# Row sums of the attention weights from a column of ones, the maximum negated where it is formed, and one cast on ScalarE

## The chip, the cores and the metric

The kernel runs on one core of one Trainium2 chip. A core has TensorE (PE; PEld is its weight load), VectorE (DVE), ScalarE (ACT), GpSimd (POOL) and SyncE (SP), which run side by side and wait for each other by semaphores. The metric is the device time of one execution in microseconds. All times below come from three timed runs of the kernel before and from one profiled execution of it.

## The reference

Two layers over 1024 latent tokens and 256 context tokens of width 1024. The first layer mixes tokens by Fourier transforms and long convolutions, the second by attention, and each ends with a gated feed-forward block. The change lies in the attention of the second layer alone: 16 heads of width 64; a query sees the keys in a window of its 16 x 64 grid, with a position bias, and all context keys, under one softmax.

```python
s_loc = einsum(q_r, k_b) * scale + bias          # masked outside the window
s_ctx = einsum(q_r, kc) * scale
s = concatenate([s_loc, s_ctx], axis=-1)
p = softmax(s, axis=-1)
o = einsum(p_loc, v_b) + einsum(p_ctx, vc)
```

## The kernel before

The program is written as Python generators, and a scheduler puts the instructions of each engine in an order by times that it works out itself; so the order on an engine is not the order of the source, and a small edit can move many instructions. Each engine then runs its own list from front to back.

**Precision.** Operands are kept as a high and a low part, and a product is three matmuls: high x high, high x low, low x high. Keys and queries are fp32r (an fp32 word rounded for TensorE), weights of the softmax and values fp16.

**Preparation.** `attn_prep(pr, u)` makes what a pair of heads `pr` (of 8) needs: keys `kk`, `kc` and queries `qs` by the linear products in `lin` (24 matmuls of 512 columns each, into PSUM tiles named `pq`), split in the lines L1989, L1990, L2002 and L2003; and values. `value(c)` loads a 128-row chunk of values (c = 0 to 3 for the four column windows of the grid, 512 columns; c = 4 for the context, 256 columns), scales it by `self.vs` into the fp16 high part on ScalarE (L1970) and takes the low part on VectorE (L1971). Both parts lie in one tile of 1024 fp16 columns. `weights` loads a weight block and splits it (L326 on ScalarE, L328 on VectorE).

**Items.** `attn_item` handles one head, half of the rows and two of the four column windows: 64 items in all (4 for each head: `hf` 0 and 1, `c0` 0 and 2). Its three stages are:

1. Scores: matmuls against 256 context keys into `pctx`, and against 384 window keys into two more PSUM tiles (`ps`). The bias tiles `g` (128 x 384) are loaded from `in_bias` by the SP queue; their pool has 4 buffers.
2. Softmax: L2072 takes the maximum of the context scores, L2075 adds the bias and takes the maximum over both (one custom instruction and a read of its accumulator), L2077 negates it, L2078 and L2080 take the exponential on ScalarE and also sum each row (each with a read of ScalarE's accumulator), L2081 adds the two sums and L2082 takes the reciprocal. Then the weights are transposed: the local ones by TensorE (L2095), split by L2098 (ScalarE, high part) and L2099 (VectorE, low part). The context's weights go another way in the first 48 items (`cross`): L2089 casts them to fp16 on VectorE, L2090 takes the low part on GpSimd, L2091 transposes both with a DMA of the SP queue. In the last 16 items they are transposed by TensorE like the others.
3. Values: 30 matmuls of 64 columns (15 for each of two windows) into one PSUM tile `o`; L2125 scales the result by the reciprocal on ScalarE. After every four items `attn_out` transposes (L2135), splits (L2137, L2138) and stores it.

`attention` walks over the items so that stage 1 of an item, stage 2 of the one before and stage 3 of the one before that stand together, and puts pieces of the next pair's preparation between them ("fill"); during the last pairs the fill is the first part of the output projection (L2390). PSUM tiles `ps` rotate over 6 banks here.

Of the kernel before, what the change touches and what calls it, by code (L numbers as in the profile page):

```python
# [12 lines left out]
F16 = mybir.dt.float16  # L13
# [5 lines left out]
P = 128  # L19
# [217 lines left out]
class Builder:  # L237
# [1664 lines left out]
    def values(self, u):  # L1902
# [31 lines left out]
        nc.vector.tensor_scalar(self.vs, m1, 8192.0, None, op0=MUL)  # L1934
        nc.vector.tensor_scalar(self.vsi, m2, 1.0 / 8192.0, None, op0=MUL)

    def attn_prep(self, pr, u):

        nc, a = self.nc, self.a
        kk = [self.S4(F32R), self.S4(F32R)]
        kc = self.S2(F32R)
        qs, vt = {}, []

        def lin(wh, wl, pc, acc, view=lambda x: x):
            acc[pc] = self.PQ()
            for kb in range(KB):
                for w, part in ((wh, 0), (wh, 1), (wl, 0)):  # L1950
                    self.mm(acc[pc][:, :WID[pc]], w[:, kb * P:(kb + 1) * P], view(u.ap(part, kb, pc)),
                            kb == 0 and w is wh and part == 0, kb == KB - 1 and w is wl)
                yield WID[pc] / 1024

        def by_chunk(x):
            return x.rearrange("p (r h c) -> p h r c", r=8, h=4)

        def value(c):
            st = self.T()
            w = 512 if c < 4 else 256  # L1960
            if c < 4:
                src = self.vd[0:LAT].rearrange("(g r w) c -> r w g c", g=4, r=4)
                for r in range(4):
                    self.ld(st[r * 32:r * 32 + 32].rearrange("p (g c) -> p g c", g=4),
                            src[r, KSTART[c]:KSTART[c] + 32, :, pr * P:(pr + 1) * P])
            else:
                self.ld(st[:, :w].rearrange("p (j c) -> p j c", j=2),
                        self.vd[LAT:LAT + CTX, pr * P:(pr + 1) * P].rearrange("(j p) c -> p j c", j=2))
            t = self.S2(F16, 1024)
            nc.scalar.activation(t[:, :w], st[:, :w], AF.Copy, scale=self.vs)  # L1970
            nc.vector.scalar_tensor_tensor(t[:, w:2 * w], st[:, :w], self.vs, t[:, :w], op0=MUL, op1=SUB)  # L1971
            vt.append(t)

        if pr == 0:
            self.aw = self.weights(a["wk"][0])
        acc = {}
        wk = self.aw
        for pc in (0, 1, 2):
            for i, s in enumerate(lin(*wk, pc, acc)):
                if i == 3:  # L1980
                    value(len(vt))
                if pc == 1 and i == 6:
                    wq = self.weights(a["wq"][pr])
                yield s
            w = WID[pc]
            for hd in (0, 1):
                own, other = slice(hd * 64, hd * 64 + 64), slice(64 - hd * 64, 128 - hd * 64)
                dst = kk[hd][:, pc * 512:pc * 512 + w] if pc < 2 else kc[:, hd * 256:hd * 256 + 256]
                nc.scalar.copy(dst[own], acc[pc][own, :w])  # L1989
                nc.vector.tensor_tensor(dst[other], acc[pc][own, :w], dst[own].bitcast(F32), SUB)  # L1990
        nxt = None
        for pc in (0, 1):
            for i, s in enumerate(lin(*wq, pc, acc, by_chunk)):
                if i == 3:
                    value(len(vt))
                if pc == 1 and i == 3 and pr < 7:
                    nxt = self.weights(a["wk"][pr + 1])
                yield s
            for hd in (0, 1):
                own, other = slice(hd * 64, hd * 64 + 64), slice(64 - hd * 64, 128 - hd * 64)  # L2000
                qh, ql = self.S2(F32R), self.S2(F32R)
                nc.scalar.mul(qh[own], acc[pc][own], 0.125)  # L2002
                nc.vector.scalar_tensor_tensor(ql[own], acc[pc][own], 0.125, qh[own].bitcast(F32), op0=MUL, op1=SUB)  # L2003
                for t in (qh, ql):
                    self.ldr(t[other].bitcast(F32), t[own].bitcast(F32))
                qs[(hd, pc)] = (qh, ql)
        self.aw = nxt
        self.prep[pr] = (qs, kk, kc, vt)
        yield 0.1
# [37 lines left out]
    def attn_item(self, head, hd, hf, c0, qs, kk, kc, vt, osb, out, cross):  # L2047
# [20 lines left out]
            loc.append(ps)  # L2068
        yield
        st = self.pt.tile([P, 16], F32, tag="st", name=self.nm("st"))  # L2070
        cm, mx, nm, s1, s2, rv = (st[:, 2 * i:2 * i + 2] for i in range(6))
        nc.vector.tensor_reduce(cm, pctx.rearrange("p (i k) -> p i k", i=2), axis=AX, op=MAX)  # L2072
        pc = self.T()
        for i in (0, 1):
            nc.vector.tensor_tensor_reduce(bias[i], loc[i][:, :384], bias[i], 1.0, cm[:, i:i + 1], ADD, MAX,  # L2075
                                           mx[:, i:i + 1])
            nc.vector.tensor_scalar(nm[:, i:i + 1], mx[:, i:i + 1], -1.0, None, op0=MUL)  # L2077
            nc.scalar.activation(pc[:, i * 256:i * 256 + 256], pctx[:, i * 256:i * 256 + 256], AF.Exp,  # L2078
                                 bias=nm[:, i:i + 1], accum_out=s2[:, i:i + 1])
            nc.scalar.activation(bias[i], bias[i], AF.Exp, bias=nm[:, i:i + 1], accum_out=s1[:, i:i + 1])  # L2080
        nc.vector.tensor_tensor(s1, s1, s2, ADD)  # L2081
        nc.vector.reciprocal(rv, s1)  # L2082
        pts = [None] * 3
        turns = [(1, bias[0], 3), (0, pc, 4), (2, bias[1], 3)]
        if cross:

            turns.pop(1)
            x, pts[0] = self.TK(F16, 1024), self.S2(F16, 1024)
            nc.vector.tensor_copy(x[:, :512], pc)  # L2089
            nc.gpsimd.tensor_tensor(x[:, 512:], pc, x[:, :512], SUB)  # L2090
            nc.sync.dma_start_transpose(pts[0].rearrange("p (n c) -> p n c", c=P), x)  # L2091
        for k, src, n in turns:
# [12 lines left out]
        for i in (0, 1):  # L2105
            c = c0 + i
            ops = []
            for g in range(3):
                gg = hf + g
                v = vt[c][:, gg * P + hd * 64:gg * P + hd * 64 + 64]  # L2110
                vl = vt[c][:, 512 + gg * P + hd * 64:512 + gg * P + hd * 64 + 64]
                ops.append((pts[1 + i], g, v, vl))
            for j in range(2):
                v = vt[4][:, j * P + hd * 64:j * P + hd * 64 + 64]
                vl = vt[4][:, 256 + j * P + hd * 64:256 + j * P + hd * 64 + 64]
                ops.append((pts[0], 2 * i + j, v, vl))
            oo = o[:, i * 64:(i + 1) * 64]
            for n, (t, j, v, vl) in enumerate(ops):
                ph, pl = t[:, j * P:(j + 1) * P], t[:, 512 + j * P:512 + (j + 1) * P]
                self.mm(oo, ph, v, n == 0, False)  # L2120
                self.mm(oo, ph, vl, False, False)
                self.mm(oo, pl, v, False, n == 4)
        for i in (0, 1):
            c = c0 + i
            nc.scalar.activation(osb[hf][:, c * P + hd * 64:c * P + hd * 64 + 64], o[:, i * 64:(i + 1) * 64],  # L2125
                                 AF.Copy, scale=rv[:, i:i + 1])
        if out is not None:
            self.attn_out(out, hf, osb[hf])
# [434 lines left out]
```

## Time and profile before

| | |
|---|---|
| median of 3 runs | 2956.7 us (2954.18 to 2958.66) |
| profiled execution | 2957.89 us, of which 2956.0 us are its span |
| granted TensorE clock, mean | 0.984 |
| busy in the span | PE 2832.5 us, DVE 2092.7, ACT 1330.1, POOL 529.2 |
| attention, 1774 to 2240 us of the span | 466 us for 64 items |
| busy in it | PE 430.09 us, DVE 359.52, ACT 315.69, POOL 118.02 |

The span is the time from the first to the last instruction; the 1.89 us between it and the time lie around it. A row of a group gives busy time, the mean of one instruction in ns, and after a second bar the idle time of the engine just before such instructions, with what ended it. A PE row shows a matmul from its issue to its modelled end, so rows overlap and a row's mean is longer than the pace at which matmuls follow each other. DVE and ACT rows overlap a little too. A row of `DVE_READ_ACCUMULATOR2_ANT` or `ACTIVATION_READ_ACCUMULATOR` is the second half of an instruction that also sums or compares along the row.

### The profile page before, as it was taken

The page shows a single profiled execution, that of the slowest core. Times are in us where ns is not written, and L with a number is a line of the kernel's source. Part 1 is how long each engine was busy: PE and PEld are TensorE (multiplying, and loading weights), DVE is VectorE, ACT ScalarE, POOL GpSimd, SP SyncE. Part 2 cuts the span into 40 slices and gives each one's busy share as a digit, 9 for nine tenths or more (in the row PEclk, how much of TensorE's full clock was granted, in tenths as well). Part 3 has the DMA queues.
Part 4 walks back from the last instruction along what each step waited for, and adds up shares of the span by engine and source line. Part 5 has one row for each costly group of instructions (what it writes and reads, how often), then busy time and mean ns, then how long its engine had stood idle before and what let it go on. Part 6 is the DMA issues. An engine that isn't in the chain of part 4 may idle for free. (4 is left out here: it accounts for less than half of the span.)

```text
span 2956.0 us, 44485 instructions
## 1 busy us (share of the span) xinstructions
PE 2832.5 (96%) x15704; PEld 2363.7 (80%) x15704; DVE 2092.7 (71%) x3950; ACT 1330.1 (45%) x2490; POOL 529.2 (18%) x820
## 2 busy tenths in 40 slices
PE   8899898899999999999999999999999999999998
PEld 3678787788799888888888888788877688888886
DVE  6765666858777888966777437888777877764555
ACT  4543323543454333333455336677665533333433
POOL 2112012351100221222120002232212022111000
PEclk9999999999999999999999999999999999999999
DMA  9664433566556555659984345676756266434653
GB/s 336 219 210 161 144 102 127 185 222 225 199 176 199 193 202 202 219 189 323 309 305 153 129 130 154 174 183 168 221 169 226 75 240 227 168 111 167 227 194 128
DMA packets 303917, 568.41 MB, mean 192 GB/s; under 512 B 83144, under 2 KB 129930, under 8 KB 303694
## 3 DMA queue, kind: packets, MB, share of 16 engines
q1 hardware_dynamic: 242750, 373.11, 39.7%
q0 software_dynamic: 58640, 188.26, 17.8%
q10 hardware_dynamic: 2304, 4.20, 0.4%
q8 instruction: 124, 2.03, 0.3%
q14 instruction: 99, 0.81, 0.1%
HBM read 415.49 MB, written 119.80 MB: 181 GB/s over the span
## 5 line engine op out<-in xcount | busy, mean ns | idle before, releaser
L1605 PE MATMUL ps<-s,s 128*128 128x512 f32 x2008 | 498.3, 391 | 6.4 <-DVE s L1496 4.7
L1605 PEld LDWEIGHTS ps<-s,s 128*128 128x128 f32 x2008 | 377.6, 188 | 88.3 <-DVE s L1496 6.3
L322 PE MATMUL ps<-s,wh 128*128 128x256 f32 (+1 forms) x1584 | 358.7, 329 | 3.5 <-ACT wh L326 3.4
L322 PE MATMUL pq<-s,wh 128*128 128x512 f32 (+1 forms) x1040 | 316.2, 381 | 9.8 <-DVE s L1990 4.7
L322 PEld LDWEIGHTS ps<-s,wh 128*128 128x128 f32 x1584 | 265.8, 192 | 29.6 <-ACT wh L326 4.7
L322 PE MATMUL ps<-s,s 128*128 128x64 f16 (+3 forms) x2780 | 243.8, 241 | 31.1 <-DVE s L2099 8.8
L1777 PE MATMUL ps<-s,s 128*128 128x512 f32 (+1 forms) x1000 | 259.6, 383 | 3.1 <-DVE s L328 3.0
L328 DVE TENSOR_TENSOR wl<-ws,wh 128x1024 fp32r<-128x1024 f32 (+1 forms) x142 | 170.0, 1198 | 127.5 <-ACT wh L326 123.0
L326 ACT CAST wh<-ws 128x1024 fp32r<-128x1024 f32 (+1 forms) x142 | 145.8, 1027 | 241.2 <-PE ps L322 91.8
L326 ACT CAST s<-s 128x1024 fp32r<-128x1024 f32 (+2 forms) x184 | 168.1, 940 | 191.3 <-DMA s<-d 162.6
L322 PE MATMUL ps<-s,wl 128*128 128x256 f32 (+1 forms) x792 | 238.4, 327 | 2.7 <-DVE wl L328 2.7
L322 PEld LDWEIGHTS pq<-s,wh 128*128 128x128 f32 x1040 | 190.8, 191 | 47.5 <-DVE s L1990 5.9
L326 ACT CAST s<-t 128x512 fp32r<-128x512 f32 (+1 forms) x213 | 121.9, 587 | 220.9 <-PE ps L1605 81.2
L328 DVE TENSOR_TENSOR s<-s,s 128x1024 fp32r<-128x1024 f32 (+2 forms) x162 | 185.5, 1177 | 49.4 <-ACT s L326 46.9
L1777 PEld LDWEIGHTS ps<-s,s 128*128 128x128 f32 x1000 | 184.5, 188 | 41.2 <-DVE s L328 4.6
L322 PE MATMUL ps<-s,mat 128*128 128x512 f32 x714 | 180.3, 402 | 18.1 <-ACT s L326 10.9
L322 PE MATMUL pq<-s,wl 128*128 128x512 f32 (+1 forms) x520 | 196.3, 379 | 1.3 <-DVE wl L328 1.3
L328 DVE TENSOR_TENSOR s<-t,s 128x512 fp32r<-128x512 f32 (+1 forms) x213 | 136.9, 653 | 78.9 <-ACT s L326 51.0
L1605 PE MATMUL ps<-s,wh 128*128 128x512 f32 x608 | 189.1, 390 | 0.0
L322 PEld LDWEIGHTS ps<-s,mat 128*128 128x128 f32 x714 | 135.6, 193 | 54.9 <-ACT s L326 13.5
L322 PEld LDWEIGHTS ps<-s,s 128*128 128x128 f32 (+1 forms) x860 | 133.9, 196 | 45.3 <-ACT s L326 10.9
L322 PEld LDWEIGHTS ps<-s,wl 128*128 128x128 f32 x792 | 148.8, 191 | 16.4 <-DVE wl L328 3.6
(439 smaller groups left out, 5614.9 us busy)
## 6 DMA issues: line engine op xcount, KB each, us to landing
s<-d SPq DMA_DIRECT2D x283, 256.0 KB, 3.8
s<-in_down SPq DMA_DIRECT2D x150, 256.0 KB, 4.1
d<-s POOLq DMA_DIRECT2D x137, 256.0 KB, 3.3
s<-in_ada_w POOLq DMA_DIRECT2D x64, 512.0 KB, 5.2
d<-tk POOLq DMA_DIRECT2D x98, 256.0 KB, 3.6
g<-in_bias SPq DMA_DIRECT2D x128, 192.0 KB, 3.1
ws<-in_up SPq DMA_DIRECT2D x44, 512.0 KB, 3.9
d<-g POOLq DMA_DIRECT2D x87, 256.0 KB, 3.1
```

What stands on the lines that cost most here:

```text
L322: self.nc.tensor.matmul(o, l, r, start=st, stop=sp)
L326: self.last_hi = nc.scalar.copy(hi, src).ins
L328: self.last_lo = eng.tensor_tensor(lo, src, hi.bitcast(F32), SUB).ins
L1605: nc.tensor.matmul(ps, x[:, sl], y, start=first and j == 0 and x is wh and y is xh, stop=j == 3 and x is wl, skip_group_check=True)
L1777: m = nc.tensor.matmul(acc[j][:, c0:c1], x[:, sl], y[:, xs], start=first and k == 0, stop=last and k == 2, skip_group_check=True)
```

## The change

Four things are done, all in the attention.

- The high part of the values gets a column of ones behind every 64 columns: `blocks(t, 65, ...)` is a view of blocks of 65, L1984 of the new file sets the ones on GpSimd, and the matmuls with the high part (two of three) have 65 columns. Column 64 of `o` is then the row's sum of weights. ScalarE no longer sums the rows, the addition L2081 is gone, and the reciprocal (now L2133) reads the sums out of PSUM after the value matmuls.
- Four blocks of 65 more columns don't fit, so `low_parts` says where the low part of a chunk lies: for c < 4 mostly in its own tile, with the last one or two blocks in the tile of the context's values. The low part of such a chunk is taken by two instructions (L1987) where it was one. The five tiles are allocated together at the start of `attn_prep`.
- The maximum is negated where it is formed: the reduction gives the negative (L2088), the custom instruction multiplies the sum by -1 and takes the minimum (L2091), the exponential of the local weights gets a scale of -1. L2077 is gone.
- The cast of the context's weights for the DMA transpose moves from VectorE (L2089) to ScalarE (L2102).

```diff
--- before.py
+++ after.py
@@ -1934,6 +1934,14 @@
         nc.vector.tensor_scalar(self.vs, m1, 8192.0, None, op0=MUL)
         nc.vector.tensor_scalar(self.vsi, m2, 1.0 / 8192.0, None, op0=MUL)
 
+    def low_parts(self, vt, c):
+
+        if c == 4:
+            return [(0, 4, vt[4][:, 260:516])]
+        if c < 3:
+            return [(0, 6, vt[c][:, 520:904]), (6, 2, vt[4][:, 516 + c * P:516 + c * P + P])]
+        return [(0, 7, vt[3][:, 520:968]), (7, 1, vt[4][:, 900:964])]
+
     def attn_prep(self, pr, u):
 
 
@@ -1955,21 +1963,29 @@
         def by_chunk(x):
             return x.rearrange("p (r h c) -> p h r c", r=8, h=4)
 
-        def value(c):
+        vt[:] = [self.S2(F16, 1024) for _ in range(5)]
+        filled = []
+
+        def value():
+            c = len(filled)
+            filled.append(c)
             st = self.T()
-            w = 512 if c < 4 else 256
+            n = 8 if c < 4 else 4
             if c < 4:
                 src = self.vd[0:LAT].rearrange("(g r w) c -> r w g c", g=4, r=4)
                 for r in range(4):
                     self.ld(st[r * 32:r * 32 + 32].rearrange("p (g c) -> p g c", g=4),
                             src[r, KSTART[c]:KSTART[c] + 32, :, pr * P:(pr + 1) * P])
             else:
-                self.ld(st[:, :w].rearrange("p (j c) -> p j c", j=2),
+                self.ld(st[:, :256].rearrange("p (j c) -> p j c", j=2),
                         self.vd[LAT:LAT + CTX, pr * P:(pr + 1) * P].rearrange("(j p) c -> p j c", j=2))
-            t = self.S2(F16, 1024)
-            nc.scalar.activation(t[:, :w], st[:, :w], AF.Copy, scale=self.vs)
-            nc.vector.scalar_tensor_tensor(t[:, w:2 * w], st[:, :w], self.vs, t[:, :w], op0=MUL, op1=SUB)
-            vt.append(t)
+            blocks = lambda x, w, b0, k: x[:, b0 * w:(b0 + k) * w].rearrange("p (b c) -> p b c", c=w)
+            t = vt[c]
+            nc.gpsimd.memset(blocks(t, 65, 0, n)[:, :, 64:65], 1.0)
+            nc.scalar.activation(blocks(t, 65, 0, n)[:, :, :64], blocks(st, 64, 0, n), AF.Copy, scale=self.vs)
+            for b0, k, lo in self.low_parts(vt, c):
+                nc.vector.scalar_tensor_tensor(blocks(lo, 64, 0, k), blocks(st, 64, b0, k), self.vs,
+                                               blocks(t, 65, b0, k)[:, :, :64], op0=MUL, op1=SUB)
 
         if pr == 0:
             self.aw = self.weights(a["wk"][0])
@@ -1978,7 +1994,7 @@
         for pc in (0, 1, 2):
             for i, s in enumerate(lin(*wk, pc, acc)):
                 if i == 3:
-                    value(len(vt))
+                    value()
                 if pc == 1 and i == 6:
                     wq = self.weights(a["wq"][pr])
                 yield s
@@ -1992,7 +2008,7 @@
         for pc in (0, 1):
             for i, s in enumerate(lin(*wq, pc, acc, by_chunk)):
                 if i == 3:
-                    value(len(vt))
+                    value()
                 if pc == 1 and i == 3 and pr < 7:
                     nxt = self.weights(a["wk"][pr + 1])
                 yield s
@@ -2068,25 +2084,22 @@
             loc.append(ps)
         yield
         st = self.pt.tile([P, 16], F32, tag="st", name=self.nm("st"))
-        cm, mx, nm, s1, s2, rv = (st[:, 2 * i:2 * i + 2] for i in range(6))
-        nc.vector.tensor_reduce(cm, pctx.rearrange("p (i k) -> p i k", i=2), axis=AX, op=MAX)
+        cm, mn, rv = (st[:, 2 * i:2 * i + 2] for i in range(3))
+        nc.vector.tensor_reduce(cm, pctx.rearrange("p (i k) -> p i k", i=2), axis=AX, op=MAX, negate=True)
         pc = self.T()
         for i in (0, 1):
-            nc.vector.tensor_tensor_reduce(bias[i], loc[i][:, :384], bias[i], 1.0, cm[:, i:i + 1], ADD, MAX,
-                                           mx[:, i:i + 1])
-            nc.vector.tensor_scalar(nm[:, i:i + 1], mx[:, i:i + 1], -1.0, None, op0=MUL)
+            nc.vector.tensor_tensor_reduce(bias[i], loc[i][:, :384], bias[i], -1.0, cm[:, i:i + 1], ADD, MIN,
+                                           mn[:, i:i + 1])
             nc.scalar.activation(pc[:, i * 256:i * 256 + 256], pctx[:, i * 256:i * 256 + 256], AF.Exp,
-                                 bias=nm[:, i:i + 1], accum_out=s2[:, i:i + 1])
-            nc.scalar.activation(bias[i], bias[i], AF.Exp, bias=nm[:, i:i + 1], accum_out=s1[:, i:i + 1])
-        nc.vector.tensor_tensor(s1, s1, s2, ADD)
-        nc.vector.reciprocal(rv, s1)
+                                 bias=mn[:, i:i + 1])
+            nc.scalar.activation(bias[i], bias[i], AF.Exp, bias=mn[:, i:i + 1], scale=-1.0)
         pts = [None] * 3
         turns = [(1, bias[0], 3), (0, pc, 4), (2, bias[1], 3)]
         if cross:
 
             turns.pop(1)
             x, pts[0] = self.TK(F16, 1024), self.S2(F16, 1024)
-            nc.vector.tensor_copy(x[:, :512], pc)
+            nc.scalar.copy(x[:, :512], pc)
             nc.gpsimd.tensor_tensor(x[:, 512:], pc, x[:, :512], SUB)
             nc.sync.dma_start_transpose(pts[0].rearrange("p (n c) -> p n c", c=P), x)
         for k, src, n in turns:
@@ -2106,23 +2119,21 @@
             c = c0 + i
             ops = []
             for g in range(3):
-                gg = hf + g
-                v = vt[c][:, gg * P + hd * 64:gg * P + hd * 64 + 64]
-                vl = vt[c][:, 512 + gg * P + hd * 64:512 + gg * P + hd * 64 + 64]
-                ops.append((pts[1 + i], g, v, vl))
+                ops.append((pts[1 + i], g, c, 2 * (hf + g) + hd))
             for j in range(2):
-                v = vt[4][:, j * P + hd * 64:j * P + hd * 64 + 64]
-                vl = vt[4][:, 256 + j * P + hd * 64:256 + j * P + hd * 64 + 64]
-                ops.append((pts[0], 2 * i + j, v, vl))
-            oo = o[:, i * 64:(i + 1) * 64]
-            for n, (t, j, v, vl) in enumerate(ops):
+                ops.append((pts[0], 2 * i + j, 4, 2 * j + hd))
+            oo = o[:, i * 65:(i + 1) * 65]
+            for n, (t, j, vc, b) in enumerate(ops):
                 ph, pl = t[:, j * P:(j + 1) * P], t[:, 512 + j * P:512 + (j + 1) * P]
+                v = vt[vc][:, b * 65:b * 65 + 65]
+                vl = next(x[:, (b - b0) * 64:(b - b0) * 64 + 64] for b0, k, x in self.low_parts(vt, vc) if b0 <= b < b0 + k)
                 self.mm(oo, ph, v, n == 0, False)
-                self.mm(oo, ph, vl, False, False)
+                self.mm(oo[:, :64], ph, vl, False, False)
                 self.mm(oo, pl, v, False, n == 4)
+        nc.vector.reciprocal(rv, o[:, :130].rearrange("p (i c) -> p i c", c=65)[:, :, 64])
         for i in (0, 1):
             c = c0 + i
-            nc.scalar.activation(osb[hf][:, c * P + hd * 64:c * P + hd * 64 + 64], o[:, i * 64:(i + 1) * 64],
+            nc.scalar.activation(osb[hf][:, c * P + hd * 64:c * P + hd * 64 + 64], o[:, i * 65:i * 65 + 64],
                                  AF.Copy, scale=rv[:, i:i + 1])
         if out is not None:
             self.attn_out(out, hf, osb[hf])
```

Counted over the whole program, VectorE loses 128 of L2077, 64 of L2081 and 48 of L2089 and gains 32 of L1987; ScalarE gains 48 casts; GpSimd gains 40 memsets; TensorE has as many instructions as before, 1280 of them with 65 columns where there were 64.

The order of the instructions moves on all engines. In the rows below a number in a name tells tiles apart: `st` is an item's small tile of maxima and sums, `ps` and `pq` are PSUM tiles, `s` and `t` working tiles, `g` a bias tile that becomes weights. `ISA` is the custom instruction of L2075 (new L2091) and the read of its accumulator.

VectorE before, in the middle of the attention. `st_19458` is item 26 (counted from 0), `st_19566` item 27; L2099 takes the low parts of items 25 (here) and 26:

```order
L2075 ISA g_19445,st_19566<-ps_19452,g_19445,st_19566 128x384
L2075 ISA st_19566 128x1
L2081 TENSOR_TENSOR st_19458<-st_19458 128x2
L2077 TENSOR_SCALAR st_19566<-st_19566 128x1 x2
L2082 RECIPROCAL st_19458<-st_19458 128x2
L2099 TENSOR_TENSOR s_4193_19379<-ps_19375,s_4193_19379 128x384
L2099 TENSOR_TENSOR s_4195_19386<-ps_19382,s_4195_19386 128x384
L1971 SCALAR_TENSOR_TENSOR s_4199_19434<-t_19429,c_16279,s_4199_19434 128x512
L2089 CAST tk_19579<-t_19568 128x512
L2081 TENSOR_TENSOR st_19566<-st_19566 128x2
L2082 RECIPROCAL st_19566<-st_19566 128x2
```

VectorE after, at the same place. `st_19325` is item 25, `st_19529` item 27, `st_19629` item 28; L2112 is what L2099 was, here of item 26, and L2019 what L2003 was:

```order
L2088 TENSOR_REDUCE st_19529<-ps_19406 128x2
L2091 ISA g_19407,st_19529<-ps_19415,g_19407,st_19529 128x384
L2091 ISA st_19529 128x1
L2091 ISA g_19411,st_19529<-ps_19418,g_19411,st_19529 128x384
L2091 ISA st_19529 128x1
L1987 SCALAR_TENSOR_TENSOR s_4113_18861<-t_19394,c_16279,s_4113_18861 128x448
L1987 SCALAR_TENSOR_TENSOR s_4114_18862<-t_19394,c_16279,s_4113_18861 128x64
L2112 TENSOR_TENSOR s_4211_19442<-ps_19438,s_4211_19442 128x384
L2112 TENSOR_TENSOR s_4213_19449<-ps_19445,s_4213_19449 128x384
L2019 SCALAR_TENSOR_TENSOR s_4216_19493<-pq_19318,s_4215_19492 64x512
L2133 RECIPROCAL st_19325<-ps_19458 128x2
L2088 TENSOR_REDUCE st_19629<-ps_19508 128x2
```

The addition, the negations and the casts are gone. The reciprocal is that of item 25 instead of item 26 or 27, and it stands behind the low parts of item 26 and ahead of the reduction of item 28.

ScalarE before: the exponentials of item 27 (`st_19566`), the high parts of item 26 (L2098) and the scaled result of item 25 (L2125).

```order
L2078 ACTIVATE t_19568,st_19566<-ps_19440,st_19566 128x256
L2080 ACTIVATE g_19441,st_19566<-g_19441,st_19566 128x384
L2078 ACTIVATE t_19568,st_19566<-ps_19440,st_19566 128x256
L2080 ACTIVATE g_19445,st_19566<-g_19445,st_19566 128x384
L2098 CAST s_4210_19480<-ps_19476 128x384
L2098 CAST s_4212_19487<-ps_19483 128x384
L2002 ACTIVATE s_4214_19529<-pq_19350 64x512
L326 CAST wh_20072<-ws_20071 128x1024
L2125 ACTIVATE s_4197_19393<-ps_19496,st_19357 128x64 x2
```

ScalarE after, one item further: the exponentials of items 28 and 29 (`st_19629`, `st_19762`) are L2093 and L2095, L2102 is the cast that is new here, L2136 scales the result of item 26, and L2111, which was L2098, makes the high parts of item 27:

```order
L2093 ACTIVATE t_19631<-ps_19508,st_19629 128x256
L2095 ACTIVATE g_19509<-g_19509,st_19629 128x384
L2093 ACTIVATE t_19631<-ps_19508,st_19629 128x256
L2095 ACTIVATE g_19513<-g_19513,st_19629 128x384
L2102 CAST tk_19638<-t_19631 128x512
L2136 ACTIVATE s_4199_19357<-ps_19571,st_19424 128x64 x2
L2111 CAST s_4230_19547<-ps_19543 128x384
L2111 CAST s_4232_19554<-ps_19550 128x384
L2093 ACTIVATE t_19764<-ps_19611,st_19762 128x256
L2095 ACTIVATE g_19612<-g_19612,st_19762 128x384
L2093 ACTIVATE t_19764<-ps_19611,st_19762 128x256
```

The cast of the context's weights stands straight behind the exponentials of its item, ahead of the scaling of an earlier item and of the high parts.

## The prediction

> **What bounds the kernel now.** The page comes first: TensorE is busy nearly all of the span.
>
> ```profile
> span 2956.0 us, 44485 instructions
> PE 2832.5 (96%) x15704; PEld 2363.7 (80%) x15704; DVE 2092.7 (71%) x3950; ACT 1330.1 (45%) x2490; POOL 529.2 (18%) x820
> ```
>
> The change touches the attention alone, so the next view is busy time by stretch: the attention, then all that follows (columns: length, busy time of PE, PEld, DVE, ACT and POOL with their instructions, granted clock, DMA share, GB/s).
>
> ```profile
> 1774.00:2240.00 466.00, 430.09 (x3938) 370.32 (x3937) 359.52 (x923) 315.69 (x928) 118.02 (x163) 0.98 0.65 180
> 2240.00:2945.00 705.00, 693.57 (x3088) 570.22 (x3086) 474.60 (x666) 285.71 (x421) 91.62 (x169) 1.00 0.51 175
> ```
>
> In the attention TensorE stands still for 466.0 - 430.1 = 35.9 us. Behind it TensorE is busy 98% of the time, so what the attention saves or loses moves the end by as much. The waits say what TensorE stood for in the attention (waiter <- releaser: us in all, times, longest).
>
> ```profile
> PE ps L322 <- DVE s L2099: 8.8, 12, 1.6
> PE ps L322 <- DVE st L2075: 6.9, 8, 2.0
> PE pq L322 <- DVE s L1990: 4.7, 5, 1.3
> PE ps L322 <- ACT t L2078: 3.5, 5, 1.1
> PE ps L2095 <- DVE s L2099: 2.8, 3, 1.7
> PE ps L2095 <- ACT g L2080: 2.3, 5, 0.8
> PE pq L322 <- DVE s L2390: 2.0, 2, 1.5
> PE ps L322 <- ACT s L2098: 1.4, 1, 1.4
> ```
>
> These are 32.4 of the 35.9 us: VectorE 8.8 + 6.9 + 4.7 + 2.8 + 2.0 = 25.2, ScalarE 3.5 + 2.3 + 1.4 = 7.2. So TensorE is the bound, and the change can win only where it shortens these waits. The groups of the attention by form give the prices.
>
> ```profile
> L2075 DVE CUSTOM_DVE_ANT_0 g<-ps,g,st 128x384 f32<-128x384 f32 x128 | 76.0, 612 | 30.1 <-DMA g<-in_bias 15.2 <-PE ps L322 9.7 <-PE ps L2095 3.1
> L2090 POOL TENSOR_TENSOR tk<-t,tk 128x512 f16<-128x512 f32 x48 | 56.1, 1169 | 104.4 <-DVE tk L2089 77.3 <-DVE st L2081 17.6 <-DVE st L2077 7.7
> L2081 DVE TENSOR_TENSOR st<-st 128x2 f32<-128x2 f32 x64 | 27.2, 424 | 29.8 <-ACT g L2080 29.3
> L2078 ACT ACTIVATION_READ_ACCUMULATOR t<-ps,st 128x1 f32 x128 | 25.3, 197 | 0.0
> L2080 ACT ACTIVATION_READ_ACCUMULATOR g<-g,st 128x1 f32 x128 | 24.9, 195 | 0.0
> L2089 DVE CAST tk<-t 128x512 f16<-128x512 f32 x48 | 23.5, 491 | 15.8 <-ACT t L2078 10.6 <-issue 3.1 <-POOL tk L2090 1.7
> L1971 DVE SCALAR_TENSOR_TENSOR s<-t,c,s 128x512 f16<-128x512 f32 x28 | 22.1, 793 | 0.6 <-ACT s L1970 0.4
> L2077 DVE TENSOR_SCALAR st<-st 128x1 f32<-128x1 f32 x128 | 16.9, 147 | 0.7
> L2082 DVE RECIPROCAL st<-st 128x2 f32<-128x2 f32 x64 | 10.4, 162 | 1.3
> L2098 ACT CAST s<-ps 128x512 f16<-128x512 f32 x16 | 9.5, 592 | 0.4 <-PE ps L2095 0.4
> L1971 DVE SCALAR_TENSOR_TENSOR s<-t,c,s 128x256 f16<-128x256 f32 x7 | 3.3, 476 | 0.0
> ```
>
> Last, the timeline of PE, DVE and ACT around one wait (start, length, engine, what, idle time before it).
>
> ```profile
> 1900.36 1.04 PE L322 MATMUL ps<-s,s 128*128 128x64 f16 x30
> 1901.23 0.42 PE L2135 MATMUL ps<-c,s 128*128 128x128 f32 x2
> 1904.59 0.98 PE L322 MATMUL ps<-s,s 128*128 128x384 f32 x2 [1.39 <-DVE s L2099]
> ...
> 1900.65 0.27 DVE L2077 TENSOR_SCALAR st<-st 128x1 f32<-128x1 f32 x2
> 1903.16 0.16 DVE L2081 TENSOR_TENSOR st<-st 128x2 f32<-128x2 f32 x1 [2.24 <-ACT g L2080]
> 1903.24 0.68 DVE L2072 TENSOR_REDUCE st<-ps 128x2 f32<-128x512 f32 x1
> 1903.84 0.16 DVE L2082 RECIPROCAL st<-st 128x2 f32<-128x2 f32 x1
> 1903.91 1.00 DVE L2099 TENSOR_TENSOR s<-ps,s 128x384 f16<-128x384 f32 x2
> ...
> 1900.91 0.47 ACT L2078 ACTIVATE t<-ps,st 128x256 f32<-128x256 f32 x1 [3.45 <-DVE st L2077]
> 1901.29 0.19 ACT L2078 ACTIVATION_READ_ACCUMULATOR t<-ps,st 128x1 f32 x1
> 1901.38 0.60 ACT L2080 ACTIVATE g<-g,st 128x384 f32<-128x384 f32 x1
> ...
> 1903.03 0.85 ACT L2098 CAST s<-ps 128x384 f16<-128x384 f32 x2
> ```
>
> The tiny addition L2081 holds VectorE for 2.24 us until ScalarE has all row sums, and the reduction behind it, whose scores were there, and the low parts L2099 come late; TensorE waits 1.39 us for the latter. VectorE runs its list in order, so L2081 is a gate. But L2099 also needs L2098, which ScalarE starts only after four exponentials. Not all waits are of this kind:
>
> ```profile
> 2123.49 0.62 DVE L2075 CUSTOM_DVE_ANT_0 g<-ps,g,st 128x384 f32<-128x384 f32 x1 [3.37 <-DMA g<-in_bias]
> ...
> 2124.17 1.01 PE L322 MATMUL ps<-s,s 128*128 128x64 f16 x29 [1.83 <-DVE st L2075]
> ```
>
> Here a bias load is late, and no edit of this change touches that load.
>
> **The change part by part.** The sum is made against the profiled execution, 2957.89 us, 1.2 us above the median of 2956.7.
>
> *VectorE's lighter list.* Gone are L2081 (27.2 us busy and 29.3 idle for ScalarE), L2077 (16.9) and L2089 (23.5): 67.6 us of work, besides the idle time, of 359.5. What this is worth lies in TensorE's waits. Those for L2099 and L1990 (8.8 + 2.8 + 4.7 = 16.3 us) end behind work of this list, and I take three quarters of them, -12 us: the timeline shows that part of such a wait is ScalarE's. Those for L2075 and L2390 I leave, since they hang on scores and loads. Bounds: 0 and -25.2.
>
> *The shorter way to the exponentials.* Without L2077 the first exponential starts 0.15 us sooner (one of the pair that took 0.27). Each accumulator read costs less than its 0.19: it starts at 1901.29 and the next exponential at 1901.38, so 0.09. By the fourth exponential that makes about 0.2 to 0.4. TensorE waited for exponentials 5 + 5 times: 10 x (0.15 + 0.2) = 3.5; I take -3, bounds 0 and -5.8 (3.5 + 2.3).
>
> *ScalarE's books.* 256 reads x 0.09 = 23 us go, and 48 casts come. The nearest row, L2098 at 128x512, has 592 ns, which with the overlap of neighbouring rows (two L2098 of 128x384 take 0.85) is about 0.5 each: 24 us. So ScalarE is not relieved; work moves to it. Queued behind the new cast are the high parts (L2111 in the new file), as the order of ScalarE shows, and TensorE waits for those through L2099. It did so 12 + 3 + 1 = 16 times in 64 items, 12 of them by share in the 48 items that have the cast; each now has 0.5 more and up to 0.36 less ahead of it: 12 x 0.15 = 1.8. I take +2; bounds 0 and 48 x 0.5 = +24. The page "ScalarE: Activation LUTs" of the Trainium skill speaks against this edit: its section "Rules for kernel authors" gives simple arithmetic to VectorE, not ScalarE, and its figures (186 ns + 0.833 ns an element) would make the cast 613 ns, an estimate; the sum by it would be 48 x 0.02 = 1 us worse. The trace agrees on the engine's own price (491 ns on VectorE against 592), but shows VectorE as the engine that TensorE waits for more.
>
> *The cast's own followers.* The low part on GpSimd (L2090) and the DMA transpose on SP wait for it. GpSimd stood idle 77.3 us for the cast on VectorE, so here a cast straight behind its exponentials can only help; the transpose reaches SP's queue sooner, and with it the bias loads behind it. I put 0; bounds -5 (a third of the 15.2 us that L2075 stood for loads) and 0.
>
> *The reciprocal.* It waits for the 30 value matmuls, which take 1901.23 - 1900.36 = 0.87 us, and then costs about 0.16 (L2082's row; it now reads PSUM). In the new order it stands, in 30 of 64 items, within four places ahead of a low part (L2112) whose transposes TensorE did just before those matmuls. The low part would have waited some 0.4 for its high part anyway, so it comes up to 0.87 + 0.16 - 0.4 = 0.6 late. TensorE waited for low parts in 15 of 64 items (12 + 3): 30 x 15/64 x 0.6 = 4.2 if nothing stands between. With fill between I take +1; bounds 0 and 30 x 1.03 = +31. ScalarE's scaling of the result comes later by the same, and nobody in the eight rows waits for that.
>
> *The 65th column.* 30 matmuls of 64 columns in 0.87 us are 29 ns each, 0.45 ns a column: 1280 x 0.45 = +0.6 us on TensorE. Bounds: 0, and twice the price, 1280 x 29 ns = +37, if a block that begins at an odd 2-byte column is read at half pace; no row shows such a read, and the nearest, at 29 ns, has even starts.
>
> *Split low parts of values.* 256 columns fewer save 793 - 476 = 317 ns, so an instruction has about 159 ns besides its columns: 32 x 0.16 = 5.1 us more on VectorE, +1 on the path at the share of the term above. The 40 memsets are put on GpSimd, idle for 348 of the 466 us, at nothing; behind them stand its DMA issues and L2090, and at L2090's price they would fill 47 us of that idle time. That the five value tiles are held from the start of a preparation is put at nothing too: the first to stand for a tile that is not free would be such a memset, under the same cover.
>
> Negating in the reduction and in L2075 changes no shape, so it costs nothing.
>
> Sum: -12 - 3 + 2 + 0 + 1 + 0.6 + 1 = -10.4 us. That gives 2947.5 for the profiled execution and 2946.3 against the median.
>
> **The rivals.** *All waits go.* With the gate L2081 away, the order may flow so well that the 32.4 us of waits go: -32.4 + 4.6 = -28, 2929. For it speaks that VectorE stands still less on ScalarE; against it the late bias loads. 0.15.
>
> *The bias loads inherit.* VectorE comes sooner to L2075 and stands there for its load instead (15.2 us now): the gain of the first two terms falls to a third, -5 + 4.6 = 0, 2956. The row at 2123.49 speaks for it. 0.14.
>
> *Slower: the reciprocal is the new gate.* VectorE now stands for TensorE where it stood for ScalarE. From the point at which TensorE has no fill between two items, each of the 30 places costs the whole 1.03 us: +31 - 15 + 3.6 = +20, 2976. The order speaks for it; that TensorE does the matmuls soon after the low parts of their own item speaks against it. 0.11.
>
> *Slower: ScalarE is the new bound.* If every one of the 48 casts delays the high parts and TensorE by its whole 0.5: +24 - 15 + 2.6 = +12, 2968. This is also where the page's rule would lead. ScalarE's 315.7 of 466 us speak against it. 0.10.
>
> That the change doesn't do what it says is excluded by the order: the instructions are gone.
>
> **How the numbers follow.** The forecast has 0.50; its own range is -4 to -20, 2937 to 2953. About 0.2% (5.9 us) is what a measurement of this kernel can tell from no change. Faster by more: 0.50 x 0.85 + 0.15 + 0.02 = 0.60. Within: 0.50 x 0.15 + 0.10 = 0.17. Slower: 0.02 + 0.11 + 0.10 = 0.23. The range reaches from the first rival to the ScalarE rival, 2926 to 2968, and leaves out the reciprocal as a full gate.
>
> **What would show it.** Right: in the attention TensorE's idle time falls from 35.9 to about 25 us, VectorE's busy time from 359.5 to about 297 (67.6 less, 5.1 more), the waits for L2099's successor fall most, and the value matmuls still start 29 ns apart. Wrong: idle time before L2133 of more than about 15 us with TensorE waiting for L2112; idle time of L2091 for bias loads well above 15.2; value matmuls slower than 29 ns apart; or a busier ScalarE with TensorE waiting for its casts.

## The result and the profile after

The changed kernel takes 2941.93 us (median of 7 runs, 2934.2 to 2946.89) against 2954.74 for the kernel before on the same chip: a ratio of 0.9946, 95% interval 0.9932 to 0.996, or 13 us less. The forecast was 10.4 us less. The profiled execution took 2940.22 us with a span of 2938.5, against 2957.89 and 2956.0 before.

Busy time by stretch of the changed kernel, attention and the rest (columns as before):

```profile
1771.00:2222.00 451.00, 422.14 (x3935) 368.08 (x3934) 311.03 (x711) 320.42 (x720) 122.11 (x199) 0.98 0.72 185
2222.00:2928.00 706.00, 694.55 (x3093) 570.78 (x3091) 476.08 (x668) 285.76 (x421) 92.07 (x170) 1.00 0.52 176
```

The attention is 15 us shorter, and what follows takes what it took. TensorE's idle time in it went from 35.9 to 28.9 us. This is what TensorE waited for in the changed kernel (L2112 was L2099, L2091 was L2075, L2006 was L1990, L2093 and L2095 were L2078 and L2080, L2136 was L2125, L2111 was L2098, L2401 was L2390):

```profile
PE ps L322 <- DVE st L2091: 12.8, 8, 3.1
PE ps L2108 <- DVE s L2112: 2.8, 4, 1.3
PE ps L322 <- ACT s L2136: 2.6, 2, 1.3
PE ps L2108 <- DVE st L2091: 1.9, 2, 1.6
PE ps L322 <- ACT t L2093: 1.7, 2, 1.3
PE pq L322 <- DVE s L2401: 1.6, 1, 1.6
PE ps L2108 <- ACT s L2136: 1.2, 3, 0.6
...
PE ps L2108 <- ACT g L2095: 0.7, 2, 0.3
PE pq L322 <- DVE s L2006: 0.6, 2, 0.3
PE ps L2146 <- ACT s L2136: 0.6, 1, 0.6
PE ps L322 <- ACT s L2111: 0.6, 1, 0.6
PE ps L322 <- DVE s L2112: 0.5, 1, 0.5
```

The waits for low parts and split keys (L2099 and L1990, 16.3 us) are down to 2.8 + 0.5 + 0.6 = 3.9. The waits for the custom instruction with the bias have doubled, 6.9 to 14.7, and those for the scaled result have grown from 1.0 to 4.4. Most of these are waits of matmuls that use nothing that L2091 or L2136 writes; by the source these two are the last to read older PSUM tiles, so the likely reading is that TensorE waits for a free tile (the rows name the releaser, not the tile). The groups by form show what holds L2091 and L2136 up:

```profile
L2091 DVE CUSTOM_DVE_ANT_0 g<-ps,g,st 128x384 f32<-128x384 f32 x128 | 76.0, 614 | 41.0 <-DMA g<-in_bias 19.3 <-PE ps L322 18.3
L322 PE MATMUL ps<-s,s 128*128 128x65 f16 x1280 | 71.1, 195 | 15.2 <-DVE st L2091 11.8 <-ACT s L2136 2.6 <-ACT s L2111 0.6
L2112 DVE TENSOR_TENSOR s<-ps,s 128x384 f16<-128x384 f32 x128 | 67.6, 551 | 40.9 <-ACT s L2111 40.2
L2136 ACT ACTIVATE s<-ps,st 128x64 f32<-128x64 f32 x128 | 33.5, 317 | 30.2 <-DVE st L2133 26.9 <-PE ps L322 3.0
L2102 ACT CAST tk<-t 128x512 f16<-128x512 f32 x48 | 29.6, 620 | 0.1
L1987 DVE SCALAR_TENSOR_TENSOR s<-t,c,s 128x384 f16<-128x384 f32 x21 | 12.9, 613 | 0.3
L1987 DVE SCALAR_TENSOR_TENSOR s<-t,c,s 128x128 f16<-128x128 f32 x21 | 10.9, 521 | 0.4 <-PE ps L2146 0.4
L2133 DVE RECIPROCAL st<-ps 128x2 f32<-128x2 f32 x64 | 10.5, 165 | 21.4 <-PE ps L322 20.9
```

VectorE no longer stands for ScalarE's sums (29.3 us at L2081), but it stands 20.9 us at the reciprocal for the value matmuls, 40.2 for the high parts (8.0 at L2099 before) and 19.3 for bias loads (15.2 before). Bias loads lie behind the two largest single waits of TensorE that are left. This is one of them:

```profile
2152.58 0.62 DVE L2091 CUSTOM_DVE_ANT_0 g<-ps,g,st 128x384 f32<-128x384 f32 x1 [3.13 <-DMA g<-in_bias]
...
2153.26 3.42 PE L322 MATMUL ps<-s,s 128*128 128x65 f16 x36 [3.10 <-DVE st L2091]
```

VectorE waits 3.13 us for a bias tile, and TensorE 3.10 behind it. Of the 14.7 us for L2091, VectorE itself was waiting for a load during 8.4 us; before it was 1.7 of 6.9.

The matmuls behind that wait are slow besides. The third number from the end of the next row is the granted clock:

```profile
2153.26:2154.90 1.64, 1.64 (x30) 1.64 (x29) 0.67 (x3) 0.97 (x3) 0.00 (x0) 0.50 0.17 62
```

At half the clock 30 value matmuls take 1.64 us; in the kernel before, at the full clock, 30 took 0.87. The last section counts these stretches.

### The profile page after: what moved, and what is told of

It reads as the page before. It is cut to its first block, busy times and chain, and to the rows that moved or that the text cites. A ratio compares the mean times of both kernels' runs of the same rounds, so it can differ in the third digit from the quotient of the medians.

```text
span 2938.5 us, 44126 instructions
## 1 busy us (share of the span) xinstructions
PE 2824.0 (96%) x15704; PEld 2361.3 (80%) x15704; DVE 2044.7 (70%) x3742; ACT 1334.5 (45%) x2282; POOL 534.0 (18%) x860
## 4 chain that ended last, share of the span: by engine, by line
PE 73%; issue 10%; DMA 8%; DVE 5%; ACT 2%; POOL 1%; SPq 1%; POOLq 0%; DVEq 0%; ACTq 0%
PE ps L1605 24%; PE ps L322 23%; PE pq L322 12%; PE ps L1777 5%; PE pq L1605 3%; PE ps L1889 2%; PE pq L1777 2%; DMA s<-d 1%; DMA g<-in_bias 1%; PE ps L2108 1%; DMA mat<-in_ada_k 1%; DMA s<-in_c_ctx 1%; PE ps L1111 1%; DMA s<-in_x_t 1%; DVE wl L328 1%
## 5 line engine op out<-in xcount | busy, mean ns | idle before, releaser
L322 PE MATMUL ps<-s,s 128*128 128x65 f16 (+4 forms) x2780 | 241.2, 240 | 25.9 <-DVE st L2091 12.8
L322 PEld LDWEIGHTS ps<-s,mat 128*128 128x128 f32 x714 | 135.8, 193 | 55.3 <-ACT s L326 13.7
```

What stands on the lines that cost most here:

```text
L322: self.nc.tensor.matmul(o, l, r, start=st, stop=sp)
```

## The experiments

Ratios are to the kernel before, run beside each. Three theories were put up: that VectorE standing at the addition L2081 was what cost (gate), that the amount of work on VectorE was (lighter list), and that any new order moves the time by chance (order). TensorE's idle time is taken from one view for all kernels, busy time of TensorE from 1770 to 2250 us, as 480 less the busy time; it is that of one profiled execution. The clock is the mean granted clock of the whole span over all runs of a kernel. For e2 and e4 the profiled execution took 2961.01 us against a median of 2946.85, and 2962.85 against 2955.75, so the rows of their traces are not typical.

| kernel | ratio, interval | TensorE idle, us | clock, mean of runs |
|---|---|---|---|
| before | 1 | 35.9 | 0.9851 |
| the change | 0.9946 [0.9932, 0.996] | 28.9 | 0.9859 |
| e1 addition queued late | 0.9931 [0.9918, 0.9945] | 27.9 | 0.9884 |
| e2 ones alone | 0.9968 [0.9954, 0.9982] | 25.6 | 0.9868 |
| e3 negation alone | 0.9930 [0.9914, 0.9946] | 23.4 | 0.9882 |
| e4 cast alone | 0.9996 [0.9985, 1.0007] | 36.0 | 0.9845 |
| f1 ones and negation | 0.9949 [0.9935, 0.9964] | 23.8 | 0.9857 |
| f2 ones and cast | 0.9969 [0.9958, 0.9979] | 27.5 | 0.9864 |
| f3 negation and cast | 0.9907 [0.9891, 0.9922] | 22.7 | 0.9885 |
| f4 negation, addition late | 0.9910 [0.9894, 0.9925] | 21.6 | 0.9868 |
| g1 the change, ones unused | 0.9938 [0.992, 0.9955] | 24.1 | 0.9855 |
| g2 the change, no reciprocal | 0.9917 [0.99, 0.9935] | 21.5 | 0.9874 |
| g3 negation, cast, addition late | 0.9913 [0.9895, 0.9931] | 20.0 | 0.9880 |
| g4 the change, 5 bias buffers | 0.9913 [0.9895, 0.9931] | 19.6 | 0.9860 |

The clock column matters for what follows. Among the 51 runs of the kernel before, a run is about 1.8 us longer for each 0.001 that its clock is lower (a fitted line); if all work went by the clock, 0.001 of 2955 us would be 3 us. Estimates of the clock's part below use these two as bounds.

**e1, the addition queued late.** `follow(low)` queues what stands in it behind the instruction `low`.

```diff
-        nc.vector.tensor_tensor(s1, s1, s2, ADD)
-        nc.vector.reciprocal(rv, s1)
...
-            nc.vector.tensor_tensor(t[:, 512:512 + w], ps[:, :w], t[:, :w], SUB)
+            low = nc.vector.tensor_tensor(t[:, 512:512 + w], ps[:, :w], t[:, :w], SUB).ins
             pts[k] = t
+        with self.follow(low):
+            nc.vector.tensor_tensor(s1, s1, s2, ADD)
+            nc.vector.reciprocal(rv, s1)
```

> The kernel before, with nothing removed: the addition of the row sums and the reciprocal are only queued on VectorE behind the low parts of their own item, when ScalarE has long finished the sums. Gate theory (VectorE standing for ScalarE's sums was what cost): 6 to 12 us faster than before, VectorE's idle time before the addition near 0 instead of 29.3 us, TensorE's waits for low parts about halved from 11.6 us. Lighter-list theory (the removed work was what cost): within 3 us of before. Order theory (any new order moves the time by chance): within 6 us either way, with no relation to the addition's idle time.

20 us faster, with not one instruction removed. Its addition L2100 by form, and of TensorE's waits the two largest and the other one for low parts:

```profile
L2100 DVE TENSOR_TENSOR st<-st 128x2 f32<-128x2 f32 x64 | 12.6, 197 | 0.0
```

```profile
PE ps L322 <- DVE st L2075: 9.0, 12, 1.2
PE ps L322 <- DVE s L2097: 2.2, 3, 0.9
...
PE ps L2093 <- DVE s L2097: 1.0, 2, 0.8
```

The idle time before the addition is gone (29.8 before), and so is more than half of its busy time (27.2), which was waiting as well, for GpSimd (last section). TensorE's waits for low parts, the rows with L2097, fell from 11.6 to 3.2 us. The lighter-list theory expected no gain here and falls; the gate theory has the direction, but the gain lies above its range of 6 to 12 us. TensorE's idle time fell by only 8 us. The granted clock accounts for another 6 to 10 us (an estimate): it was 0.988 or 0.989 in all five runs, and 0.981 to 0.987 in the 23 of the kernel before beside them.

**e2, ones alone.** The change without the negation and without the cast on ScalarE.

> The kernel before with the column of ones alone; negations and cast stay on VectorE. Gate theory: 7 to 12 us faster, most of the whole change. Lighter-list theory: of 50.7 us of real work that the change takes off VectorE (64 x 0.161 for the addition, 16.9, 23.5) this part has 10.3, so 2 to 3 us faster. Order theory: no relation, within 6 us either way.

9 us faster (0.9968), as the gate theory expected and more than the lighter list gives. But it takes the gate away as e1 does and has only half of e1's gain.

**e3, negation alone.**

```diff
-        nc.vector.tensor_reduce(cm, ..., axis=AX, op=MAX)
+        nc.vector.tensor_reduce(cm, ..., axis=AX, op=MAX, negate=True)
...
-                                           mx[:, i:i + 1])
-            nc.vector.tensor_scalar(nm[:, i:i + 1], mx[:, i:i + 1], -1.0, None, op0=MUL)
+                                           nm[:, i:i + 1])
```

> The kernel before with the maximum negated where it is formed, and nothing else. Gate theory: 1 to 3 us faster, from a way to the exponentials that is 0.15 us shorter. Lighter-list theory: 16.9 of 50.7 us, 4 us faster. Order theory: within 6 us either way.

20 us faster, far beyond every expectation. The exponential of the local weights also gets a scale of -1, as in the change; the diff here is shortened. The addition is still there (L2080 in this kernel), and stands less:

```profile
L2080 DVE TENSOR_TENSOR st<-st 128x2 f32<-128x2 f32 x64 | 25.6, 400 | 17.4 <-ACT g L2079 17.2
```

```profile
PE ps L322 <- DVE st L2075: 4.8, 6, 2.2
PE ps L322 <- DVE s L2098: 3.4, 5, 0.9
...
PE ps L2094 <- DVE s L2098: 0.4, 1, 0.4
```

With the exponentials started sooner, VectorE is idle 17.4 us at the addition instead of 29.8, and TensorE's wait for low parts is 3.4 + 0.4 = 3.8 instead of 11.6. The clock is as high as in e1, which is 6 to 9 of the 20 us (an estimate). How much of the rest is the shorter standing and how much the new order is not settled.

**e4, cast alone.** L2089 becomes `nc.scalar.copy(x[:, :512], pc)`.

> The kernel before with the context's cast on ScalarE, and nothing else; the row sums are still read from ScalarE's accumulator, so here ScalarE only gets more work (about 24 us). Gate theory: 0 to 4 us slower, since the cast can stand ahead of work that the gate waits for. Lighter-list theory: 23.5 of 50.7 us, 6 us faster. ScalarE rival of the prediction: 5 to 15 us slower. Order theory: within 6 us either way.

No change (0.9996): 23.5 us of work taken off VectorE bought nothing, which the lighter-list theory can't explain, and ScalarE's additional work cost nothing. Yet in its trace VectorE stands at the addition for ScalarE 47.8 us, 29.3 before: more standing, and no more time. It is also the one kernel with a new order and no gain; no kernel was run with a new order alone, so chance by the order is not excluded for a few us in the others.

**f1 to f4, the pairs.** f1 is the change with the cast back, f2 the change with the negations back, f3 is e3 and e4 together, f4 is e3 and e1 together.

> The changed kernel with the context's cast back on VectorE: column of ones and negation. The earlier runs: negation alone about 20 us faster than before, ones alone about 9, cast alone within 2 us. If the cast on ScalarE is what holds the whole change back (ScalarE theory), this is 5 to 10 us faster than the changed kernel, about 0.993 of before. If the column of ones takes back (reciprocal theory: VectorE stands for TensorE's value matmuls), it is within 3 us of the changed kernel, about 0.995. If parts add, 0.990.

> The changed kernel with the negations back: column of ones and cast on ScalarE. ScalarE theory: slower than ones alone (0.997), about 0.998 to 1.001. Reciprocal theory: as ones alone, 0.996 to 0.998.

> The kernel before with negation and the cast on ScalarE, row sums still by ScalarE's accumulator. ScalarE theory: 5 to 10 us slower than the negation alone (0.993), so 0.995 to 0.997. Reciprocal theory: as the negation alone, 0.992 to 0.994.

> The kernel before with the negation and with the addition and reciprocal queued behind the low parts; row sums still by ScalarE, cast on VectorE. If the two cure different waits they add: 0.985 to 0.989, faster than the changed kernel and than each alone. If both cure the same wait (VectorE standing in the addition for the exponentials), no faster than the better one: 0.992 to 0.994.

f1 is 0.9949 and as fast as the whole change; f2, at 0.9969, is as fast as ones alone; f3 is 0.9907 and no slower than the negation alone. So the ScalarE theory falls three times, and f3 is faster than the reciprocal theory had it too (0.992 to 0.994). With the three edits on and off the column of ones shows both faces: it is worth -0.0032 alone and -0.0027 beside the cast; beside the negation the difference is +0.0019, within the intervals; beside negation and cast it costs +0.0039 (11.5 us), where the intervals of f3 and of the change are apart. f4 has a ratio 0.002 below e1 and e3, which the intervals don't tell apart, and lies between its two expectations, far from the sum of their gains.

f3 also bears on the gate theory. This is its addition:

```profile
L2080 DVE TENSOR_TENSOR st<-st 128x2 f32<-128x2 f32 x64 | 18.3, 287 | 30.3 <-ACT g L2079 30.0
```

VectorE stands there for ScalarE as long as before the change (30.0 and 29.3 us), and f3 is among the fastest. So the standing need not cost anything; what differs is whether TensorE waits for what is queued behind it. Its waits for low parts are 11.6 us before and 7.6 in e4, but 2.6 in f3, 3.2 in e1 and 3.8 in e3.

**g1 and g2, what of the column of ones costs.** g1 keeps the column and its layout, but takes the sums from `accum_out` again, with addition and reciprocal in their old place:

```diff
+                                 bias=mn[:, i:i + 1], accum_out=s2[:, i:i + 1])
+            nc.scalar.activation(bias[i], bias[i], AF.Exp, bias=mn[:, i:i + 1], scale=-1.0, accum_out=s1[:, i:i + 1])
+        nc.vector.tensor_tensor(s1, s1, s2, ADD)
+        nc.vector.reciprocal(rv, s1)
...
-        nc.vector.reciprocal(rv, o[:, :130].rearrange("p (i c) -> p i c", c=65)[:, :, 64])
```

> The changed kernel, column of ones, split low parts and all, but the sums come from ScalarE's accumulator again, with the addition and the reciprocal where they stood before; the column of ones is computed and not used. Beside it stands negation with cast (0.991 of before), which differs only in the layout of the values. If the late reciprocal is what costs (reciprocal theory): as negation with cast, 0.989 to 0.993. If the layout costs (65 columns, split low parts, memsets): as the changed kernel, 0.994 to 0.996.

> The changed kernel with the reciprocal left out: the result is scaled by a constant instead of by one over the row sum, so nothing on VectorE waits for the value matmuls, and nothing sums the rows for use. Reciprocal theory: 8 to 15 us faster than the changed kernel, 0.989 to 0.992 of before. Layout theory: within 3 us of the changed kernel, 0.994 to 0.996.

g2, which scales by a constant and has no reciprocal, gives 0.9917, 8.6 us better than the change: the lower end of what the reciprocal theory expected. g1 gives 0.9938, between the two expectations, and 0.0031 worse than f3, from which it differs in the layout alone. So both the late reciprocal and the layout seem to cost; each interval just touches the one it is compared with, and their sizes don't add up to the 0.0039. Much of these differences is the clock: g1's is 0.0030 below f3's, 5 to 9 us (an estimate) of a difference of 9, and g2's is 0.0015 above the change's, 3 to 5 of 8.6. Which of them costs how much stays open.

**g3, negation, cast and late addition.**

> Negation, cast on ScalarE, and the addition and reciprocal queued behind the low parts; no column of ones. The pairs of these were 0.9907 (negation and cast) and 0.9910 (negation and late gate). If the three still add: 0.986 to 0.989, the fastest version. If what is left of the waits is bias loads, which none of the three touches: 0.990 to 0.992.

0.9913: the late addition adds nothing to negation and cast. It takes away VectorE's 30.0 us of standing in f3, and the time stays: TensorE hardly waited for what was behind it any more.

**g4, five bias buffers.** `pg` gets 5 buffers and `p2` 34 in the changed kernel.

> The changed kernel with five bias buffers instead of four, paid for by one working tile fewer (34 instead of 35). Bias theory (the waits for the custom instruction that adds the bias, the largest left in the changed kernel, come from late bias loads): these waits fall by half from 14.7 us, 4 to 8 us faster than the changed kernel, 0.992 to 0.993 of before. If the loads are late because of what stands ahead of them on SP's queue and not for want of a buffer: within 3 us of the changed kernel.

0.9913, 9.8 us faster than the change, somewhat above the 4 to 8 us of the bias theory, at the same clock. Its other number failed:

```profile
L2091 DVE CUSTOM_DVE_ANT_0 g<-ps,g,st 128x384 f32<-128x384 f32 x128 | 75.1, 614 | 31.4 <-PE ps L322 25.1 <-DMA g<-in_bias 2.7
```

```profile
PE ps L322 <- DVE st L2091: 12.3, 10, 2.8
```

VectorE waits for bias loads 2.7 us instead of 19.3, so the loads were late for want of a buffer, and the working tile given up for it cost nothing that shows. But TensorE's wait for L2091 only goes from 14.7 to 12.8 (the row above, and one of 0.5). The part of it in which VectorE itself waits for a load falls from 8.4 to 2.1 us; in its place come ten waits of 0.5 to 1.3 us without a load behind them. The other waits of TensorE fell too, and all idle time goes from 28.9 to 19.6 us. VectorE is now there sooner and stands for TensorE's scores (25.1).

f3, f4, g3 and g4 all beat the changed kernel by some 10 us and don't differ from each other by what their intervals can tell. f3 is the smallest edit: two of the change's three parts, without the column of ones.

## Why the prediction was right

The forecast was -10.4 us and the result -13; direction and size held, and the waits that it said would fall fell. Of the mechanism only a part held, and that the sum fits is partly luck: by its own steps it missed new waits and a gain in busy time that nearly cancel.

- *VectorE's lighter list*, -12: the waits for L2099 and L1990 fell by 16.3 - 3.9 = 12.4. The size holds, the name does not: e1 gets these waits down with nothing removed, and e4 removes 23.5 us of work and gains nothing. Some 17 of the 67.6 us called work were VectorE waiting for GpSimd inside the row of L2081 (last section).
- *The shorter way to the exponentials*, -3: 5.8 to 1.7 + 0.7 = 2.4 us, so -3.4 by the waits. By e3 the negation alone is worth 20 us of time, with less standing at L2081, fewer waits for low parts and a higher clock; the term was too narrow.
- *ScalarE's books*, +2: the wait for L2111 is 0.6 where L2098's was 1.4, and e4 puts the move at nothing. The cast took 620 ns. The page "ScalarE: Activation LUTs" of the Trainium skill gives 613 by its figures (an estimate), so price and row agree. Its rule under "Rules for kernel authors" names `relu`, `max`, `min`, `add` and `mul` for VectorE and not a cast; carried over to the cast, as the prediction did, it made no difference in e4 either way (0.9996).
- *The reciprocal*, +1: "nobody in the eight rows waits for that" failed. The waits for the scaled result are 2.6 + 1.2 + 0.6 = 4.4 us, where before two small rows outside the eight had 1.0; ScalarE stands 26.9 for the reciprocal, VectorE 20.9 for the matmuls (the prediction's own sign of being wrong was 15, with waits for L2112, which fell instead), and g2 is 8.6 us faster without it, part of it clock. This is the rival of the new gate in small, and the term most mis-sized.
- *"Those for L2075 and L2390 I leave"* failed for L2075: 6.9 became 14.7, and of the 7.8 us more, 6.7 are waits in which VectorE itself waits for a load. This is the rival of the bias loads, come true beside the forecast, and g4 shows what a buffer is worth.
- *The 65th column*: matmuls of 65 columns have the same mean as those of 64 before, 195 ns, and still start 29 ns apart (median); an odd start costs nothing that the rows show.
- *Split low parts*: for 21 of the 28 large chunks 613 + 521 ns where one took 793, so 341 ns more and not 159; for the other 7, 682 + 280, which is 169 more. Four of the 21 small instructions stood beside GpSimd's L2103 and took 1262 ns; the other 17 took 346. VectorE's busy time was forecast at 297 and is 311. The rows summed up fell by 59 us, near the forecast's 62.5, but they overlap less than before.

The idle rows add up to 7.0 us less, but the attention is 15 us shorter. The other 8 us are in TensorE's busy time, 430.09 to 422.14 for nearly as many instructions (3938 and 3935). Some 3 of them are the clock: the stretches at half the clock in the attention add up to 20.5 us before and 13.7 after, and half of the difference is 3.4 us (an estimate). What the other 5 are is not shown; waits hidden under the modelled ends of rows are one candidate. The prediction took its sum from idle rows alone, with no term for the clock, and missed +11 of new waits and -8 of busy time.

## What to carry to other kernels

A tiny instruction that waits for another engine can cost more than the large ones around it, since all that is queued behind it waits too. Its own idle time doesn't tell: it was 30 us in the kernel before and in one of the fastest. Look whether the engine that bounds the kernel waits for what is queued behind it, and try first to queue it later, which here gave as much as the whole change with nothing removed. Before a difference of some us is put down to an edit, compare the granted clock of all runs. Parts of a change that cure the same wait don't add up, and one that replaces a gate by another can turn from a gain to a loss once the first gate is gone; run them apart and in pairs.

## What the runs showed of the hardware

A wait can count as busy time, and here it is a wait for GpSimd. Before the change the addition of two columns had this spread (min, median, max):

```profile
L2081 DVE TENSOR_TENSOR st<-st x64: 145/161/1545, 1786.8 to 2227.9; 128x2 f32<-128x2 f32 x64
```

and in f4, where it hardly waits, this mean:

```profile
L2099 DVE TENSOR_TENSOR st<-st 128x2 f32<-128x2 f32 x64 | 10.4, 163 | 0.0
```

So of the 27.2 us before, some 17 were waiting that the row shows as work. The trace tells for what:

```profile
1786.80 1.10 DVE L2081 TENSOR_TENSOR st<-st 128x2 f32<-128x2 f32 x1 [0.17 <-ACT g L2080]
...
1786.72 1.17 POOL L2090 TENSOR_TENSOR tk<-t,tk 128x512 f16<-128x512 f32 x1 [9.91 <-DVE tk L2089]
```

The idle time before the addition ended with ScalarE's sums; the addition itself ends when GpSimd's subtraction L2090 ends. That is so for all 20 of the 64 additions that took over 200 ns: each ends 14 to 27 ns after an L2090. The addition reads two operands from SBUF. VectorE's L2099, which reads one of its two from PSUM, shows nothing of the kind: 18 that ran beside an L2090 took 547 ns, the other 110 took 550. So part of what e1 cured was not a wait for ScalarE.

The granted clock of TensorE falls to half in short stretches. In the attention before the change there are four, of 3.4, 6.8, 6.8 and 3.4 us, and in the changed kernel three, of 3.4, 3.4 and 6.8 us. One of the kernel before:

```profile
2068.44:2075.27 6.83, 6.17 (x48) 5.94 (x49) 5.79 (x16) 4.97 (x16) 2.28 (x3) 0.50 0.42 133
```

All seven begin within a wait of TensorE of more than 1 us or at most 1.4 us behind one. So a wait may cost more than its own length; but that the wait brings the stretch about is not shown, and in e1 nine waits of 1.0 to 1.9 us are followed by none:

```profile
1770.00:2250.00 480.00, 452.12 (x4073) 386.52 (x4072) 368.72 (x963) 334.24 (x958) 126.65 (x179) 1.00 0.70 189
```

In e4 the same row has a clock of 0.96, with TensorE idle as long as before (36.0 and 35.9 us):

```profile
1770.00:2250.00 480.00, 444.01 (x3982) 381.51 (x3981) 338.56 (x883) 343.89 (x982) 122.66 (x170) 0.96 0.67 177
```

But that is one execution, of 2962.85 us; over all runs e4's clock is that of the kernel before (0.9845 and 0.9851), so the row says nothing of the cast. Over all runs the clock differs between kernels where e1, e3 or f3 is compared with the kernel before; why is open.
